# Moving h, queries, keys and y to other SBUF offsets, with two local reorderings and two adds on GpSimd, in a two-layer decoder trunk

## The chip, the cores and the metric

The kernel runs on one core of a Trainium2 chip, in one launch. The metric is the device time of that launch in microseconds (us). Before the change it is 455.19 us, the median of three executions (455.1, 455.19 and 544.2 us). The five engines are called PE (matrix multiply; PEld is its weight load), DVE (VectorE), ACT (ScalarE), POOL (GpSimd) and SP (SyncE, which here issues most DMAs).

## The reference

A trunk of two layers on x of 256 tokens by 1024 channels, all in float32. Each layer takes h = rmsnorm(x) * (1 + scale) + shift, where scale, shift and gate come from c through a matrix (`ada_w`), runs a mixer, and adds gate * y to x. Layer 0 of the reference (here "layer 1") is sparse attention, layer 1 ("layer 2") is an mLSTM:

```python
for i in range(2):
    shift, scale, gate = jnp.split(c @ ada_w[i] + ada_b[i], 3, axis=-1)
    h = rmsnorm(x, norm_g[i]) * (1.0 + scale[:, None, :]) + shift[:, None, :]
    y = nsa_mixer(h, ...) if i == 0 else mlstm_mixer(h, ...)
    x = x + gate[:, None, :] * y
return rmsnorm(x, final_g)
```

`nsa_mixer` projects h to queries (16 heads of 64), six key and value sets (4 groups of 64), gate logits and z. One key set and one value set are compressed: blocks of 32 tokens, each with a position row added (`blocks + pe`), go through a small network. Three attention branches (compressed, selected, sliding; at 256 tokens the last two are causal attention over their own keys and values) are mixed by sigmoid gates, multiplied by silu(z) and projected by `w_out`. `mlstm_mixer` projects h to q, k (with a causal convolution), v, two gates, an output gate and z, runs a gated linear recurrence and projects again.

## The kernel before

**Precision.** A float32 product is made of three matmuls on `float32r` operands. Each factor is split into a high part (rounded by ACT, L165) and a low part (the rest, by DVE, L170); the three are high x high, high x low and low x high. For h these parts are `hh` and `hl`, each 128 partitions x 8 x 256 (8 blocks of 128 channels, 256 tokens). For weights they are `wh` and `wl`, tiles of 1024 columns in rings of six.

**Stream.** SP loads the weights in pieces of up to 512 KB into a ring of ten `raw` tiles (L88) in one fixed order; a piece is issued as soon as the tile that it takes has been read for the last time. `split_next` splits the next piece.

**Layer 1** is written in program order for PE, ACT, DVE and SP (`manual_schedule`); POOL is not in that list. `first_phase` makes the columns of scale and shift from `ada_w`, modulates h block by block (L440, L448) and multiplies each block with the weights of queries and keys: L476, 336 matmuls, the weights stationary, 256 columns of h moving. `evac_cmp` copies the keys and values to be compressed into tiles E and `embed` adds the position rows (L546): two adds for each of E[0] and E[1], all four on DVE. `nsa` finishes the projections: `gemm_tok` (L566 to L568: h stationary, weights moving), `gemm_ws` (L1674 to L1676: weights stationary, 256 columns of h moving), `hidden` (L602: the network of the compressed tokens). Attention runs in eight units n. `S(n)` makes scores (L970 with 256 columns and L974 with 512, queries stationary, keys moving) and DVE turns them into a masked minimum form (L984); `softmax(n)` takes the exponentials on ACT (L996); `factors` and `scaled(n, j)` apply the gates on DVE (L1004 to L1013); `T_pair(n, j)` transposes on PE (L1026) and ACT copies the result out (L1028, tile PT); `PV(n)` multiplies with the values (L1048, L1040). The four `z_steps` are 48 `gemm_ws` matmuls each. `gate_steps` makes half of the residual gate in four steps: rows on PE (L227), a copy on ACT (L938), a matmul on PE (L941), an add on DVE (L944). `cmp_tokens(a)` transposes the compressed scores on PE (L735) into PSUM bank 3, and DVE reads them out (L736); both calls use that bank. y takes the place of the queries, and `out_mm` (L881, 96 matmuls with 512 columns of weights moving, y stationary) makes the output projection.

**The turn and layer 2.** `turn` adds the residual, makes the second h into the same tiles and begins layer 2 (L1279). Layer 2 uses `gemm_tok` with 512 columns, `gemm_ws` for q and k, and in `project` the final product L1165 (y stationary, 512 or 256 columns of weights moving). Its order is set by the framework's scheduler.

**Before the first product** `warm(9)` and `idle` run matmuls whose results nobody reads. `idle` (L255) multiplies a zeroed tile `quiet` with itself 12 times: `float32r`, 512 columns, the stationary part 64, 96, 160, 192, 224 and 384 bytes (mod 512) behind the moving part, twice each.

Of the kernel before, what the change touches and what calls it, by code (L numbers as in the profile page):

```python
# [7 lines left out]
F32 = mybir.dt.float32  # L8
F32R = mybir.dt.float32r
# [3 lines left out]
OP = mybir.AluOpType  # L13
# [10 lines left out]
class Kernel:  # L24
# [225 lines left out]

    def idle(self, w, gaps, i=7):
        z = self.quiet
        b = self.bank(i)
        for c in gaps:
            self.nc.tensor.matmul(b[:, 0:w], z[:, 512 + c : 512 + c + P], z[:, 0:w], start=True, stop=True)  # L255

    def setup(self):
        nc, t, pc = self.nc, self.t, self.pc
        self.x = self.T(pc, [P, 2, D])
        self.hh = self.T(pc, [P, KC, SEQ], F32R)  # L260
        self.hl = self.T(pc, [P, KC, SEQ], F32R)
        xr = t["x"][0].rearrange("(a p) d -> p a d", p=P)
# [10 lines left out]
        nc.vector.memset(still, 0.0)  # L273
        self.quiet = self.T(self.p1, [P, KC * SEQ], F32R, tag="xT")
        nc.vector.memset(self.quiet[:, 0:1024].bitcast(F32), 0.0)
        self.warm(9)
# [72 lines left out]


    def layer1(self):
        nc, t, pc, p1 = self.nc, self.t, self.pc, self.p1
# [49 lines left out]
    def first_phase(self, place):  # L402
# [4 lines left out]
        nc.tensor.transpose(bt[:, 0:32], self.prc, ident[:32, :32])  # L407
        self.idle(512, [n for n in (16, 24, 40, 48, 56, 96) for _ in range(2)])
        pca = self.pca = self.T(pc, [P, 96])
# [6 lines left out]
        xT = self.T(p1, [P, KC, SEQ], tag="xT")  # L416
        ss = self.T(p1, [P, 2], tag="ss2")
        nc.scalar.activation(ss[:, 0:1], self.eps, AF.Sqrt)
        xn = [self.T(p1, [P, D], tag=tag) for tag in ("KH", "KL")]
        for a in range(2):  # L420
            nc.scalar.activation(xn[a], self.x[:, a], AF.Square, accum_out=ss[:, a : a + 1])
# [105 lines left out]
    def evac_cmp(self, accs):  # L527

        nc, p1 = self.nc, self.p1
        self.E, self.F = [], {}  # L530
        for n, acc in enumerate(accs):
            E = self.T(p1, [P, 4, 17, 8], tag="tz", bufs=2)
            self.E.append(E)
            nc.vector.memset(E[:, :, 16], 0.0)
            src = acc.rearrange("p (c x r) -> p c r x", c=2, r=2)
            for half in range(2):
                for par in range(2):
                    dst = E[64 * par : 64 * par + 64, half::2, 0:16].rearrange("p c s u -> p c (s u)")
                    nc.scalar.activation(dst, src[64 * half : 64 * half + 64, :, par], AF.Copy)
            self.embed(n, 0)  # L540

    def embed(self, n, o):

        F = self.F[n, o] = self.T(self.p1, [P, 8, 4, 16], tag="PT", bufs=4)
        pe = self.pca[:, 32 + 16 * n + 8 * o : 40 + 16 * n + 8 * o]
        self.nc.vector.tensor_tensor(F.rearrange("p u g s -> p g s u"), self.E[n][:, :, o : 16 + o], pe.unsqueeze(1).unsqueeze(1).to_broadcast([P, 4, 16, 8]), op=OP.add)  # L546

# [22 lines left out]
    def nsa(self, acc):  # L570
# [70 lines left out]
        hidden(1)  # L641
        for n in range(2):
            self.embed(n, 1)
        vg_block(1)
# [82 lines left out]
        cmp_scores(1)  # L727
        self.scaled(1, 1)
        self.softmax(2, (0,))
        Tc = self.T(p1, [P, 2, 16, 16], tag="tz", bufs=2)  # L730

        def cmp_tokens(a):
            b = self.bank(3)
            for i in range(4):
                nc.tensor.transpose(b[:, i * P : i * P + P], St[i // 2][:, i % 2, a * P : a * P + P], ident)  # L735
            nc.vector.tensor_tensor(Tc[:, a].rearrange("p (i g) s -> p i g s", i=4), b.rearrange("p (i g s) -> p i g s", i=4, g=4)[:, :, :, 0:16],  # L736
                                    self.slc.unsqueeze(2).unsqueeze(3).to_broadcast([P, 4, 4, 16]), op=OP.mult)

        self.PV(0)
        cmp_tokens(0)  # L740
        self.T_pair(1, 0)
        nc.scalar.dma_start(self.gate0, t["ada_b"][0:1, 2048:3072].partition_broadcast(P))
# [59 lines left out]
        g1 = self.gate_steps(1, 3)  # L802
        self.go(g1, 2)

        self.T_pair(3, 0)
        self.go(g1, 2)
        self.split_next()
        self.T_pair(3, 1)
        self.split_next()
        self.factors(4)  # L810
        self.scaled(4, 0)
        self.S(5)
        self.gated(0, 1)
        self.scaled(4, 1)
        self.softmax(5)
        self.PV(3)
        self.gated(1, 0)
        z = self.z_steps(2)
# [385 lines left out]
    def turn(self):  # L1204
        nc, pc, p1, pieces = self.nc, self.pc, self.p1, self.pieces
        halves = [slice(0, 512), slice(512, D)]
        ss = [self.T(pc, [P, 3], tag="ss", bufs=2) for _ in range(2)]
# [182 lines left out]
    def layer2(self):  # L1390
        nc, t, pc, p2, ident = self.nc, self.t, self.pc, self.p2, self.ident
        pcb = self.pcb
        g = nc.gpsimd

        V = self.T(p2, [P, 2, 8, 258], F32R, tag="V")
        VL = [self.T(p2, [P, 2, 258], F32R, tag=f"num{h}") for h in range(8)]
        NUM = {}
        den = self.T(p2, [P, 2, 8])
        g.memset(V.bitcast(F32)[:, :, :, 256:258], 1.0)
# [79 lines left out]
        QK = self.T(p2, [P, 16, SEQ], tag="QK")  # L1479
        ss = self.T(p2, [P, 2, 8])  # L1480

# [236 lines left out]
```

## Time and profile before

| | |
|---|---|
| median of the runs | 455.19 us |
| the profiled execution | 455.72 us |
| its span in the trace | 453.9 us |
| PE, PEld busy | 442.2 us (97%), 373.5 us (82%) |
| DVE, ACT, POOL busy | 328.5 us, 268.0 us, 35.8 us |
| DMA | 95.63 MB, 211 GB/s in the mean |
| granted PE clock | full in all 40 slices |

Times in the trace count from the start of the span. A row of the timeline has the start in us, the time from that start to the end of the last of the merged instructions, engine, line, operation, tiles (out<-in), shape and count; in brackets stand the idle time of the engine before it and what ended it. Matmuls are pipelined: the time of one is its latency, and the pace is the distance from start to start. In the chain of waits a row is start, time and what, and for back-to-back matmuls time over count is the pace.

### The profile page before, as it was taken

Reading aid. Unit: us, or ns where it says so; the run is one execution under the profiler, and the core shown is the slowest. Engines: PE = TensorE matmul, PEld = TensorE weight load, DVE = VectorE, ACT = ScalarE, POOL = GpSimd, SP = SyncE. Lnnn points to the kernel's source line nnn. Section 1 sums busy time; section 2 is a strip of 40 time slices with the busy share of each in tenths; the row PEclk is TensorE's granted clock in tenths of the full one; section 3 lists DMA queues with packets and bytes.
Section 4 is the critical chain, followed back from the end, with each engine's and each line's share of the span. In section 5 each row is a group of like instructions: output and inputs, shape, how many; then the busy total and the mean of one; then the engine's idle time right before and its main releaser. Section 6 shows DMA issues by size and latency. Waiting matters only on the chain.

```text
span 453.9 us, 8341 instructions
## 1 busy us (share of the span) xinstructions
PE 442.2 (97%) x3046; PEld 373.5 (82%) x3046; DVE 328.5 (72%) x761; ACT 268.0 (59%) x527; POOL 35.8 (8%) x100
## 2 busy tenths in 40 slices
PE   8899999999999999999999999999999999999993
PEld 4788998887758877788899889988888888888883
DVE  4555579777869777587998369688986978454635
ACT  4433478675597687356857585555655555454624
POOL 8840022000000000012000000000000000000000
PEclk9999999999999999999999999999999999999999
DMA  8999999982187999897999999887845799740002
GB/s 277 371 330 319 331 357 276 274 315 84 50 269 234 268 240 294 262 202 146 255 142 107 108 303 293 172 153 232 262 141 197 200 225 247 256 139 1 0 1 92
DMA packets 71452, 95.63 MB, mean 211 GB/s; under 512 B 4540, under 2 KB 49908, under 8 KB 71412
## 3 DMA queue, kind: packets, MB, share of 16 engines
q1 hardware_dynamic: 69684, 92.73, 75.7%
q0 software_dynamic: 1392, 1.58, 1.8%
q10 hardware_dynamic: 336, 0.80, 0.5%
q8 instruction: 24, 0.39, 0.4%
q14 instruction: 16, 0.13, 0.1%
HBM read 93.00 MB, written 1.05 MB: 207 GB/s over the span
## 4 chain that ended last, share of the span: by engine, by line
PE 81%; DMA 6%; DVE 4%; ACT 3%; SPq 2%; issue 2%; ACTq 0%
PE bank L568 9%; PE bank L566 8%; PE bank L567 8%; PE bank L1165 8%; PE bank L476 7%; PE bank L1674 5%; PE bank L1675 5%; PE bank L1676 5%; PE bank L881 5%; DMA raw<-in_a_w_in 5%; PE bank L1279 4%; PE bank L227 3%; PE bank L1026 2%; PE bank L1048 2%; SPq L88 2%; PE bank L1512 2%
## 5 line engine op out<-in xcount | busy, mean ns | idle before, releaser
L165 ACT ACTIVATE wh<-raw 128x1024 fp32r<-128x1024 f32 (+5 forms) x126 | 120.8, 977 | 92.4 <-DMA raw<-in_a_w_in 28.5
L170 DVE TENSOR_TENSOR wl<-raw,wh 128x1024 fp32r<-128x1024 f32 (+5 forms) x126 | 139.8, 1123 | 46.9 <-ACT wh L165 46.1
L566 PE MATMUL bank<-wh,one 128*128 128x512 f32 (+2 forms) x208 | 77.0, 371 | 0.0
L567 PE MATMUL bank<-wl,one 128*128 128x512 f32 (+2 forms) x208 | 76.4, 367 | 0.0
L568 PE MATMUL bank<-wh,one 128*128 128x512 f32 (+2 forms) x208 | 76.3, 368 | 0.0
L1674 PE MATMUL bank<-one,wh 128*128 128x256 f32 x208 | 59.6, 286 | 0.0
L1675 PE MATMUL bank<-one,wh 128*128 128x256 f32 x208 | 59.1, 284 | 0.0
L1676 PE MATMUL bank<-one,wl 128*128 128x256 f32 x208 | 59.1, 284 | 0.0
L566 PEld LDWEIGHTS bank<-wh,one 128*128 128x128 f32 x208 | 39.2, 189 | 7.0 <-ACT wh L165 0.4
L568 PEld LDWEIGHTS bank<-wh,one 128*128 128x128 f32 x208 | 39.2, 188 | 6.1
L567 PEld LDWEIGHTS bank<-wl,one 128*128 128x128 f32 x208 | 39.2, 189 | 5.9
L1674 PEld LDWEIGHTS bank<-one,wh 128*128 128x128 f32 x208 | 39.8, 191 | 1.4 <-issue 0.8
L1675 PEld LDWEIGHTS bank<-one,wh 128*128 128x128 f32 x208 | 39.9, 192 | 0.1
L1676 PEld LDWEIGHTS bank<-one,wl 128*128 128x128 f32 x208 | 39.8, 191 | 0.0
L476 PE MATMUL bank<-one,wh 128*128 128x256 f32 x224 | 30.9, 285 | 0.9 <-ACT one L440 0.9
L476 PEld LDWEIGHTS bank<-one,wh 128*128 128x128 f32 x224 | 28.3, 191 | 1.8 <-ACT one L440 1.3
L996 ACT ACTIVATE Pr<-Pr,mn 128x128 f32<-128x128 f32 (+1 forms) x64 | 28.2, 448 | 2.4 <-DVE mn L984 2.4
L1165 PE MATMUL bank<-wl,QK 128*128 128x512 f32 (+1 forms) x80 | 28.2, 353 | 0.0
L1165 PE MATMUL bank<-wh,V 128*128 128x512 f32 (+1 forms) x80 | 28.0, 350 | 0.0
L1165 PE MATMUL bank<-wh,QK 128*128 128x512 f32 (+1 forms) x80 | 28.0, 350 | 0.0
L1493 DVE SCALAR_TENSOR_TENSOR conv<-bank,one,conv 128x255 f32<-128x255 f32 (+2 forms) x48 | 20.3, 475 | 2.1 <-ACT conv L1488 2.1
L984 DVE CUSTOM_DVE_ANT_0 Pr<-bank,one 128x128 f32<-128x128 f32 (+1 forms) x64 | 18.4, 354 | 4.3 <-PE bank L970 4.3
(325 smaller groups left out, 762.4 us busy)
## 6 DMA issues: line engine op xcount, KB each, us to landing
raw<-in_b_w_in SPq DMA_DIRECT2D x62, 512.0 KB, 8.0
raw<-in_ada_w SPq DMA_DIRECT2D x34, 512.0 KB, 6.0
raw<-in_b_w_out SPq DMA_DIRECT2D x16, 512.0 KB, 5.7
raw<-in_a_w_in SPq DMA_DIRECT2D x12, 512.0 KB, 8.1
Q<-in_ada_w SPq DMA_DIRECT2D x8, 512.0 KB, 7.0
raw<-in_a_cmp_w SPq DMA_DIRECT2D x8, 512.0 KB, 8.5
raw<-in_a_w_in SPq DMA_DIRECT2D x16, 256.0 KB, 4.1
raw<-in_a_w_out SPq DMA_DIRECT2D x16, 256.0 KB, 8.6
```

Of the source, the lines that this page charges most:

```text
L165: self.nc.scalar.activation(v(hi), src, AF.Copy)
L170: self.nc.vector.tensor_sub(v(lo), src, v(hi).bitcast(F32))
L476: nc.tensor.matmul(out, w[:, ch * P : ch * P + P], h[:, kk], start=(kk == 0 and m == 0 and ch % 2 == 0), stop=(kk == 7 and m == 2), skip_g ...
L566: nc.tensor.matmul(out, self.hh[:, kk, sl], wh, start=first, stop=False, skip_group_check=True)
L567: nc.tensor.matmul(out, self.hh[:, kk, sl], wl, start=False, stop=False, skip_group_check=True)
L568: nc.tensor.matmul(out, self.hl[:, kk, sl], wh, start=False, stop=last, skip_group_check=True)
L881: nc.tensor.matmul(out, l[:, sl], w[:, c0:c1], start=(k == 0 and m == 0), stop=(k == 7 and m == 2), skip_group_check=True)
L996: self.nc.scalar.activation(v, v, AF.Exp, bias=mn[:, a, br, j : j + 1], scale=-1.0, accum_out=sm[:, a, br, j : j + 1])
L1165: ins = nc.tensor.matmul(out, l[:, sl], w[:, c0:c1], start=(k == 0 and m == 0), stop=(k == N - 1 and m == 2), skip_group_check=True)
L1674: nc.tensor.matmul(out, wh, self.hh[:, kk], start=first, stop=False, skip_group_check=skip)
L1675: nc.tensor.matmul(out, wh, self.hl[:, kk], start=False, stop=False, skip_group_check=skip)
L1676: nc.tensor.matmul(out, wl, self.hh[:, kk], start=False, stop=last, skip_group_check=skip)
```

## The change

Four things are done. Where the lines of code move, the profile's line numbers of the changed kernel differ by a few from those of before.

1. **Offsets.** `hh` and `hl` become two views of one tile `hbuf`, 80 columns longer than the two; layer 1 uses it from column 0, layer 2 from column 80 (`h_views`). Small tiles are padded, or made earlier, so that other tiles shift. The addresses in the two built programs give the distance from the moving to the stationary operand, mod 512 bytes:

| matmuls | columns moving | before | changed |
|---|---|---|---|
| L476 (336), `gemm_ws` of layer 1 (48 for keys, 192 in `z_steps`) | 256 | 256 | 64 |
| `gemm_tok` of layer 1, values (48) | 256 | 256 | 448 |
| `gemm_tok` of layer 1, 304 columns (48) | 304 | 64, 256, 384 | 64, 256, 448 |
| all h products of layer 2, L1279 among them | 256, 512 | 256 | 256 |
| L970 (32), L974 (32): keys against queries | 256, 512 | 0 | 256 |
| L881 (96): y against weights | 512 | 320 (72), 0 (24) | 256 |
| L1165 (144): y against weights | 512 | 448 (96), 0 (48) | 256 |
| L1165 (96) | 256 | 448 (64), 0 (32) | 256 |

2. **Start.** `idle` and the zeroing of its tile on DVE (L275) go; `warm(6)` stands in its place, six bf16 matmuls of 512 columns.

3. **Position rows.** The two second adds of `embed` (o = 1) go from DVE, where they stood in `nsa` behind `hidden(1)`, to POOL, right behind the first two.

4. **Two orders in layer 1.** `scaled(1, 1)` goes behind `cmp_tokens(0)`. In the second gate half, `go(g1, ...)` runs one step before `T_pair(3, 0)`, one behind `T_pair(3, 1)` and two behind `PV(3)`, and `S(5)` goes ahead of `T_pair(3, 1)`.

```diff
     def setup(self):
-        self.hh = self.T(pc, [P, KC, SEQ], F32R)
-        self.hl = self.T(pc, [P, KC, SEQ], F32R)
+        self.hbuf = self.T(pc, [P, 2 * KC * SEQ + 80], F32R)
+        self.h_views(0)
...
-        self.quiet = self.T(self.p1, [P, KC * SEQ], F32R, tag="xT")
-        nc.vector.memset(self.quiet[:, 0:1024].bitcast(F32), 0.0)
+    def h_views(self, c0):
+        n = KC * SEQ
+        self.hh, self.hl = (self.hbuf[:, c0 + n * m : c0 + n * m + n].rearrange("p (k t) -> p k t", k=KC) for m in range(2))
     def first_phase(self, place):
-        self.idle(512, [n for n in (16, 24, 40, 48, 56, 96) for _ in range(2)])
+        self.warm(6)
...
-        ss = self.T(p1, [P, 2], tag="ss2")
+        ss = self.T(p1, [P, 56], tag="ss2")[:, 0:2]
...
+        self.T(p1, [P, 64])
     def evac_cmp(self, accs):
-            self.embed(n, 0)
+            self.embed(n, 0, nc.vector)
+        for n in range(2):
+            self.embed(n, 1, nc.gpsimd)
     def nsa(self, acc):
         hidden(1)
-        for n in range(2):
-            self.embed(n, 1)
...
         cmp_scores(1)
-        self.scaled(1, 1)
         self.softmax(2, (0,))
...
         cmp_tokens(0)
+        self.scaled(1, 1)
         self.T_pair(1, 0)
...
         g1 = self.gate_steps(1, 3)
-        self.go(g1, 2)
+        self.go(g1, 1)
         self.T_pair(3, 0)
-        self.go(g1, 2)
+        self.S(5)
         self.split_next()
         self.T_pair(3, 1)
+        self.go(g1, 1)
         self.split_next()
         self.factors(4)
         self.scaled(4, 0)
-        self.S(5)
...
         self.PV(3)
+        self.go(g1, 2)
     def turn(self):
+        self.h_views(80)
     def layer2(self):
+        den = self.T(p2, [P, 64])[:, 0:16].rearrange("p (a h) -> p a h", a=2)
         V = self.T(p2, [P, 2, 8, 258], F32R, tag="V")
-        den = self.T(p2, [P, 2, 8])
+        ss = self.T(p2, [P, 32])[:, 0:16].rearrange("p (a h) -> p a h", a=2)
...
-        ss = self.T(p2, [P, 2, 8])
```

**PE around the second gate half and S(5).** Rows are line, operation, tiles and size. Before, from the second transpose group of `T_pair(3, 0)` (the first L1026) on:

```order
L1026 MATMUL bank_1844<-one_19_94,Pr_1671 128x128 x3
L941 MATMUL bank_1850<-adaA_1836,one_21_99 128x512
L1026 MATMUL bank_1869<-one_19_94,Pr_1672 128x128 x3
L1026 MATMUL bank_1875<-one_19_94,Pr_1672 128x128 x3
L970 MATMUL bank_1897<-KH_972,Q_1106 128x256
L970 MATMUL bank_1897<-KL_973,Q_1106 128x256
L970 MATMUL bank_1897<-KH_972,Q_1106 128x256
L970 MATMUL bank_1897<-KL_973,Q_1106 128x256
L974 MATMUL bank_1898<-KH_972,Q_1106 128x512
L974 MATMUL bank_1898<-KL_973,Q_1106 128x512
L974 MATMUL bank_1899<-KH_972,Q_1106 128x512
L974 MATMUL bank_1899<-KL_973,Q_1106 128x512
```

Changed, from the same transposes on (L1025, L969, L973 and L1047 are the former L1026, L970, L974 and L1048):

```order
L1025 MATMUL bank_1834<-one_16_91,Pr_1663 128x128 x3
L969 MATMUL bank_1840<-KH_968,Q_1102 128x256
L969 MATMUL bank_1840<-KL_969,Q_1102 128x256
L969 MATMUL bank_1840<-KH_968,Q_1102 128x256
L969 MATMUL bank_1840<-KL_969,Q_1102 128x256
L973 MATMUL bank_1841<-KH_968,Q_1102 128x512
L973 MATMUL bank_1841<-KL_969,Q_1102 128x512
L973 MATMUL bank_1842<-KH_968,Q_1102 128x512
L973 MATMUL bank_1842<-KL_969,Q_1102 128x512
L1025 MATMUL bank_1879<-one_16_91,Pr_1664 128x128 x3
L1025 MATMUL bank_1885<-one_16_91,Pr_1664 128x128 x3
L1047 MATMUL bank_1795<-PT_1832,one_189_970 64x256
```

The eight score matmuls went ahead of the six transposes of `T_pair(3, 1)`; the first matmul of `PV(3)` now follows those transposes at once, and the gate matmul (L941, now L940) stands behind `PV(3)`, just ahead of `z_steps(2)`.

**DVE around the compressed tokens.** Before: the eight scalings of unit 1 (L1013) and the two reads of bank 3 (L736).

```order
L1013 TENSOR_SCALAR Pr_1341<-Pr_1341,f_1503 128x128
L1013 TENSOR_SCALAR Pr_1341<-Pr_1341,f_1503 128x256
L1013 TENSOR_SCALAR Pr_1341<-Pr_1341,f_1503 128x128
L1013 TENSOR_SCALAR Pr_1341<-Pr_1341,f_1503 128x256
L1013 TENSOR_SCALAR Pr_1342<-Pr_1342,f_1503 128x128
L1013 TENSOR_SCALAR Pr_1342<-Pr_1342,f_1503 128x256
L1013 TENSOR_SCALAR Pr_1342<-Pr_1342,f_1503 128x128
L1013 TENSOR_SCALAR Pr_1342<-Pr_1342,f_1503 128x256
L736 TENSOR_TENSOR tz_1529<-bank_1539,one_49_189 128x256
L736 TENSOR_TENSOR tz_1529<-bank_1558,one_49_189 128x256
```

Changed (L1012 and L733 are the same two):

```order
L1012 TENSOR_SCALAR Pr_1333<-Pr_1333,f_1495 128x128
L1012 TENSOR_SCALAR Pr_1333<-Pr_1333,f_1495 128x256
L1012 TENSOR_SCALAR Pr_1333<-Pr_1333,f_1495 128x128
L1012 TENSOR_SCALAR Pr_1333<-Pr_1333,f_1495 128x256
L733 TENSOR_TENSOR tz_1517<-bank_1527,one_46_186 128x256
L1012 TENSOR_SCALAR Pr_1334<-Pr_1334,f_1495 128x128
L1012 TENSOR_SCALAR Pr_1334<-Pr_1334,f_1495 128x256
L1012 TENSOR_SCALAR Pr_1334<-Pr_1334,f_1495 128x128
L1012 TENSOR_SCALAR Pr_1334<-Pr_1334,f_1495 128x256
L733 TENSOR_TENSOR tz_1517<-bank_1550,one_46_186 128x256
```

The read of the first half of the compressed scores went ahead of the last four scalings.

**POOL between the two zero fills and the key copies.** Before (the L560 rows are DMAs, which copy keys to the other half of the partitions):

```order
L764 MEMSET adaA_1628 128x512
L764 MEMSET adaA_1629 128x512
L560 DMA KH_972<-KH_972 64x2x256 x2
L560 DMA KL_973<-KL_973 64x2x256 x2
L560 DMA KH_972<-KH_972 64x2x256 x2
```

Changed:

```order
L762 MEMSET adaA_1620 128x512
L762 MEMSET adaA_1621 128x512
L546 TENSOR_TENSOR PT_940<-tz_924,one_50_202 128x64x8
L546 TENSOR_TENSOR PT_942<-tz_932,one_50_202 128x64x8
L560 DMA KH_968<-KH_968 64x2x256 x2
L560 DMA KL_969<-KL_969 64x2x256 x2
```

The two adds stand on POOL ahead of the four key-copy DMAs of the first key set. What follows from these moves on the other engines: on DVE the 16 instructions that read the scores of S(5) (L984, now L983) go ahead of the four weight splits (L170) that stood in front of them, and the second add of the gate half (L944, now L943) goes behind `scaled(4, 1)`; on ACT the second gate copy (L938, now L937) goes behind the four copies of `T_pair(3, 0)` and `T_pair(3, 1)` (L1028). Layer 2 keeps its order.

More of the change, by code (lines that the diff above doesn't have):

```diff
@@ L249, in warm @@
             self.nc.tensor.matmul(b, self.still[:, 0:P], self.still, start=True, stop=True)
[L251 to L255, printed above, removed]
     def setup(self):
@@ L539, in evac_cmp, with embed @@
                     nc.scalar.activation(dst, src[64 * half : 64 * half + 64, :, par], AF.Copy)
-            self.embed(n, 0)
-    def embed(self, n, o):
+            self.embed(n, 0, nc.vector)
+        for n in range(2):
+            self.embed(n, 1, nc.gpsimd)
+    def embed(self, n, o, eng):
         F = self.F[n, o] = self.T(self.p1, [P, 8, 4, 16], tag="PT", bufs=4)
         pe = self.pca[:, 32 + 16 * n + 8 * o : 40 + 16 * n + 8 * o]
-        self.nc.vector.tensor_tensor(F.rearrange("p u g s -> p g s u"), self.E[n][:, :, o : 16 + o], pe.unsqueeze(1).unsqueeze(1).to_broadcast([P, 4, 16, 8]), op=OP.add)
+        eng.tensor_tensor(F.rearrange("p u g s -> p g s u"), self.E[n][:, :, o : 16 + o], pe.unsqueeze(1).unsqueeze(1).to_broadcast([P, 4, 16, 8]), op=OP.add)
     def dup_split(self, K, br, acc):
```

## The prediction

> **What bounds the kernel now.** I read the profile's page first: span, busy shares and the timeline in 40 slices (one digit for 11.3 us).
>
> ```profile
> span 453.9 us, 8341 instructions
> PE 442.2 (97%) x3046; PEld 373.5 (82%) x3046; DVE 328.5 (72%) x761; ACT 268.0 (59%) x527; POOL 35.8 (8%) x100
> DMA  8999999982187999897999999887845799740002
> ```
>
> PE is busy for 97% of the span. So two things can shorten the kernel: a PE wait that goes, or a smaller distance from one matmul to the next. The digits of DMA add the limit: nines up to about 90 us, then a gap around 110. What feeds PE differs before and after that gap. The chain and the timeline show it at its edge (start, time, what):
>
> ```profile
> 71.37 12.14 DMA raw<-in_a_w_in
> 83.59 1.06 ACT L165 ACTIVATE wh<-raw 128x1024 fp32r<-128x1024 f32 x1 [4.68 <-DMA raw<-in_a_w_in]
> 84.69 1.23 DVE L170 TENSOR_TENSOR wl<-raw,wh 128x1024 fp32r<-128x1024 f32 x1 [1.82 <-ACT wh L165]
> 84.09 0.28 PE L970 MATMUL bank<-KH,Q 128*128 128x256 f32 x1
> 96.47 1.07 PE L1026 MATMUL bank<-one,Pr 128*128 128x128 f32 x6 [0.73 <-DVE Pr L1013]
> ```
>
> A weight piece lands at 83.51. ACT has waited 4.68 us for it, DVE 1.82 us for ACT, and DVE's queue from there on (the splits, the reads of the first scores, the scalings L1013) ends in a PE wait of 0.73 us at 96.47. Up to that point the transfers set the time: a faster PE waits longer there. Behind it the largest PE waits are these two, each a single instruction:
>
> ```profile
> 133.29 1.13 PE L941 MATMUL bank<-adaA,one 128*128 128x512 f32 x2 [0.69 <-ACT adaA L938]
> 111.07 0.66 PE L735 MATMUL bank<-one,y 128*128 128x128 f32 x4 [0.60 <-DVE tz L736]
> ```
>
> Apart from these PE runs back to back to the end, so there a nanosecond per matmul counts.
>
> **Paces.** The distance from start to start depends on the shape and, in these rows, on the offset. First and last start of evenly spaced stretches (for L476, L974 and the bf16 probes, a chain or merged row):
>
> ```profile
> 33.54 8.50 PE bank L476 x71
> 443.97 0.28 PE L1165 MATMUL bank<-wh,QK 128*128 128x256 f32 x1
> 446.68 0.28 PE L1165 MATMUL bank<-wh,V 128*128 128x256 f32 x1
> 224.37 0.39 PE L567 MATMUL bank<-wl,one 128*128 128x512 f32 x1
> 229.35 0.39 PE L568 MATMUL bank<-wh,one 128*128 128x512 f32 x1
> 183.11 0.40 PE L881 MATMUL bank<-wl,Q 128*128 128x512 f32 x1
> 188.24 0.40 PE L881 MATMUL bank<-wh,Q 128*128 128x512 f32 x1
> 439.13 0.40 PE L1165 MATMUL bank<-wh,QK 128*128 128x512 f32 x1
> 118.58 0.92 PE bank L974 x4
> 9.24 1.03 PE L249 MATMUL bank<-y 128*128 128x512 bf16 x4
> ```
>
> - 256 columns at offset 256 (L476): 8.50 / 71 = 119.7 ns. At 448 and 0 (the tail of L1165, 23 distances): 2.71 / 23 = 117.8 ns.
> - 512 columns at 256 (layer 2, 22 distances): 4.98 / 22 = 226.4 ns. At 320 (L881, 22): 5.13 / 22 = 233.2. At 448 and 0 (L1165, 21, from 439.13 to 443.97): 230.5. At 0 (L974): 0.92 / 4 = 230. bf16, which has half the bytes: (1.03 - 0.38) / 3 = 216, with the last one's latency of about 0.38 taken off.
>
> So 256 is the best offset seen for 512 columns, but not for 256 columns. The trace has no 256-column product at 64.
>
> **Offsets, late part.** *Known pairs.* L881: 72 matmuls go from 320 to 256, 72 x 6.8 ns = -0.49 us. L974: 32 x 3.6 = -0.12. L1165: 144 x 4.1 = -0.59 with 512 columns, and 96 x 1.9 = +0.18 with 256 columns (448 and 0 to 256): -0.41. *Unknown: 64 for 256 columns.* Of such products, 192 in `z_steps` lie behind 96.47. Bounds per matmul: a gain of 119.7 - 216 / 2 = 11.7 ns (all that it exceeds half a bf16 product) to a loss of 6.8 ns (the worst difference between two offsets above). I take the nearest row, the 256-column product that isn't at 256: a gain of 1.9 ns, 192 x 1.9 = -0.36. Sum late: -1.38.
>
> **Offsets, early part.** 336 products L476 and 48 for keys, 384 x 1.9 = 0.73 us, all ahead of 96.47. I count nothing: the transfers hide it, and the wait of 0.73 should grow to about 1.4. If that cover were gone, it would be -0.73. The 96 `gemm_tok` products of layer 1 (448 for 256) change by +-4 ns at most, 0.4 us, under the same cover.
>
> **`cmp_tokens`.** The chain is: transposes (L735), DVE's read of bank 3, the second transposes.
>
> ```profile
> 108.75 1.93 DVE L1013 TENSOR_SCALAR Pr<-Pr,f 128x128 f32<-128x128 f32 x8
> 110.59 0.42 DVE L736 TENSOR_TENSOR tz<-bank,one 128x256 f32<-128x256 f32 x1
> ```
>
> The read (0.42) stood behind eight scalings that took 1.93 us; now it stands behind four and starts near 109.8, when the first transposes end. The wait of 0.60 goes: -0.60. Late next are the other four scalings, by the 0.42 of the read, and behind them T_pair(1, 1), which has the second transposes and the `gemm_ws` after them as cover.
>
> **Gate half and S(5).**
>
> ```profile
> 131.72 0.87 PE L1026 MATMUL bank<-one,Pr 128*128 128x128 f32 x6
> 136.41 1.52 PE L1048 MATMUL bank<-PT,one 128*64 128x256 f32 x16
> 137.76 1.03 PE L1040 MATMUL bank<-one,one 128*64 128x256 f32 x8
> 139.07 0.28 PE L1676 MATMUL bank<-one,wl 128*128 128x256 f32 x1
> 135.06 2.56 DVE L170 TENSOR_TENSOR wl<-raw,wh 128x512 fp32r<-128x512 f32 x4
> 167.43 0.87 PE L1026 MATMUL bank<-one,Pr 128*128 128x128 f32 x6
> 168.24 1.84 PE L1048 MATMUL bank<-PT,one 128*64 128x256 f32 x16
> 170.00 0.66 PE L1693 MATMUL bank<-one,adaA 128*128 128x128 f32 x4
> L984 DVE CUSTOM_DVE_ANT_0 Pr<-bank,one 128x128 f32<-128x128 f32 (+1 forms) x64 | 18.4, 354 | 4.3 <-PE bank L970 4.3
> ```
>
> The matmul L941 waited 0.69 us for ACT's copy; now it comes some 4 us later, behind `PV(3)`, and the copy, though behind four PT copies, is long done: -0.69. In its place PV(3) (L1048) follows the transposes at once and must wait for ACT to copy their result. A unit in which this is already so is at 167.43: its PV took 170.00 - 168.24 = 1.76 us, against 137.76 - 136.41 = 1.35 for PV(3) before. So +0.41 (bounds 0, and 1.1 if both copies queue). Behind it PE holds the rest of PV(3), L941 and `z_steps(2)`, and DVE waits for these. Net -0.28.
>
> On DVE the reads of S(5) go ahead of four splits: eight reads of 0.354, 2.8 us, of which the third has to wait until T_pair(3, 1) has read the tile that it writes, near 134.4. So the splits start near 136.2 instead of 135.06, and the first is ready about 136.9. PE reads it (L1676) at 139.07 before, now about 138.4: 1.5 us of cover. If that were gone it would cost the remainder of 1.1 us.
>
> **Position rows.**
>
> ```profile
> 78.37 2.02 DVE L546 TENSOR_TENSOR PT<-tz,one 128x512 f32<-128x512 f32 x2
> 199.97 1.66 POOL L1197 TENSOR_TENSOR one<-one,y 128x512 f32<-128x512 f32 x1 [123.01 <-DVE y L1196]
> 201.12 1.06 DVE L1197 TENSOR_TENSOR one<-one,y 128x512 f32<-128x512 f32 x1
> 202.55 0.68 DVE L1270 TENSOR_TENSOR one<-tz,one 128x512 fp32r<-128x512 f32 x1
> 68.08 2.25 DVE L170 TENSOR_TENSOR wl<-raw,wh 128x1024 fp32r<-128x1024 f32 x2
> 70.60 0.28 PE L1676 MATMUL bank<-one,wl 128*128 128x256 f32 x1
> 66.29 1.31 POOL L560 DMA_DIRECT2D KH<-KH  x2 [7.88 <-ACT KH L555]
> KH<-KH POOLq DMA_DIRECT2D x4, 128.0 KB, 6.8
> ```
>
> DVE is freed of 2.02 us, but then it waits 1.82 us for ACT and the transfer at 84.69, so nothing is gained. On POOL an add of this size took 1.66 us, two 3.3. They stand ahead of the key copies (four DMAs, 2 x 1.31 us of issue from 66.29, 6.8 us each to land): landed by 76 before, by 79 at the worst, read at 84.09. Zero, if DVE isn't held up meanwhile (a rival below).
>
> **Start.** The probes go and six bf16 products stand there. PE waits for DVE at the end of both:
>
> ```profile
> 8.39 0.64 PE L227 MATMUL bank<-raw,one 128*32 128x128 f32 x16 [0.24 <-DVE rq_y L215]
> ```
>
> So zero; DVE's zero fill of 128x1024 comes off its own chain, with at most the 0.4 us that the transfers then take back.
>
> **Sum.** -1.38 - 0.60 - 0.28 = -2.26 us. The profiled execution took 455.72 (span 453.9 and 1.8 around it): 453.46. It lay 0.53 above the median of the three runs, 455.19, so the median should be 452.9. That is 0.5% faster; 2% is 9.1 us, about what a measurement of this kernel can tell from no change.
>
> **Rivals.**
>
> *The offset does nothing.* The paces differ by shape and place in the program (what is loaded next, which banks), not by the offset. For it: even the 119.7 and 117.8 stand in different layers. Against it: L881 is the same loop as a 512-column product of layer 2 and slower by 6.8 ns. Then only the two waits count, -0.88: 455.72 - 0.88 - 0.53 = 454.3.
>
> The Trainium skill ("TensorE: Matmul & The Clock Gate", Part 2, What happens when you issue a matmul) says that PE has two independent SBUF read ports and that loading the next weights takes no read bandwidth from the running product. By that rule this rival is what comes. The trace doesn't agree well: 226.4 against 233.2 at one shape.
>
> *The adds on POOL hold up DVE.* While POOL added (199.97 to 201.63), a DVE add that read two SBUF tiles took 1.06 us, beside 0.68 for the same size just after. If the two new adds each hold back DVE's splits, which stand close there, by their whole 1.66, PE's next weights come 3.3 us late. The first of the two splits from 68.08 is ready near 69.2 and first read at 70.60, a lead of some 1.3; with 0.73 of wait at 96.47 that leaves +1.3 on the forecast, 454.2. The Trainium skill ("SBUF — State Buffer", SBUF: two separate sides) calls the port pair of the two engines an exclusive lock for a whole instruction; those 1.06 us agree.
>
> *64 is a bad place.* If 64 costs 6.8 ns, as 320 does against 256, then the 192 late products lose 1.31 us and the 384 early ones 2.61, of which 0.73 goes into the wait at 96.47. With the other offsets (-1.02) and the waits (-0.88): 1.31 + 1.88 - 1.90 = +1.29, 456.5, slower than before. It decides from 4.6 ns on, where 0.576 x - 0.73 = 1.90. Against it: nothing at 256 columns lies above 119.7.
>
> *64 is much better.* Half of the 11.7, 6 ns: 0.79 us more in the late part, and of the early 2.3 us half gets through, because earlier reads also free `raw` tiles earlier for the stream: 452.9 - 0.8 - 1.15 = 451.0.
>
> **How the numbers follow.** Forecast 0.55, no effect of the offset 0.17, POOL 0.10, 64 bad 0.07, 64 much better 0.11. The range takes in the first three and the last, and the bounds of the wait of PV(3) (-0.4, +0.7): 450.4 to 455.6; it leaves out the bad 64 and the ends of the bounds. No case reaches 2%: within 2% 0.96, and 0.02 on either side for what no row shows.
>
> **What would show it.** Right: the 71 L476 of the chain at about 8.37 us; the 36 L881 of a stretch shorter by 0.16 to 0.25; no wait at the former L735 and L941; a new PE wait of some 0.4 at PV(3) on ACT's PT; the wait near 96 about 1.4 long. Wrong: L476 at 8.50 or more (no effect, or a bad place); a wait near 96 that stays at 0.7 with everything earlier (the early part isn't the transfers'); DVE splits over 1.3 us beside the POOL adds with a PE wait behind them; or PE waits at `z_steps(2)` for its weights.

## The result and the profile after

The changed kernel takes 452.6 us (median of 5 executions), against 455.1 before (5 executions): ratio 0.9946, 95% interval 0.9929 to 0.9963, that is 2.5 us or 0.5% less. One execution of each five (2458.2 and 544.2 us) was disturbed and is left out of the ratio. The profiled execution took 451.9, 0.7 under its median, so its trace flatters the change: 3.8 us lie between the two traces, 2.5 between the medians. Which part of the 3.8 is the change's is the main question of the experiments.

The first lines of the page:

```profile
span 450.1 us, 8331 instructions
PE 438.0 (97%) x3040; PEld 369.6 (82%) x3040; DVE 326.5 (73%) x758; ACT 268.3 (60%) x527; POOL 39.1 (9%) x102
```

PE is 4.2 us less busy, at the same share. The list of PE's waits (us in total, times, longest):

```profile
PE bank L227 <- DMA raw<-in_ada_w: 2.3, 1, 2.3
PE bank L249 <- DVE y L267: 1.2, 1, 1.2
PE bank L227 <- DMA Q<-in_ada_w: 0.6, 1, 0.6
PE bank L474 <- ACT one L438: 0.5, 2, 0.3
PE bank L227 <- DVE xT L927: 0.3, 1, 0.3
```

The three waits that the prediction named (at the former L1026, L735 and L941) are gone. The new 2.3 us stand at the start: with the shorter warm-up PE is idle earlier and waits at the same product L227, which now starts at 8.90 us instead of 8.39. The wait of 0.3 on `xT` (at 120.69) is new as well; it is taken up with the two orders at the end.

The paces, from the chain of waits (start, time, what):

```profile
33.26 8.06 PE bank L474 x71
58.62 5.80 PE bank L474 x49
179.26 8.38 PE bank L880 x36
```

and the last of these before:

```profile
182.84 8.54 PE bank L881 x36
```

L474 (formerly L476), now 64 bytes from its weights: 8.06 / 71 = 113.5 ns, where it was 119.7. But this is a fast stretch: the 49 from 58.62 take 5.80 / 49 = 118.4. Over all distances between neighbours in the trace the mean is 114.8, against 119.6 before; the z steps have 115.6 against 119.6. The 36 L880 (formerly L881) are 0.16 shorter, as 24 products x 6.8 ns. The two orders, first PE around the compressed tokens:

```profile
106.42 1.01 DVE L1012 TENSOR_SCALAR Pr<-Pr,f 128x128 f32<-128x128 f32 x4
107.58 0.42 DVE L733 TENSOR_TENSOR tz<-bank,one 128x256 f32<-128x256 f32 x1 [0.15 <-PE bank L732]
107.92 1.00 DVE L1012 TENSOR_SCALAR Pr<-Pr,f 128x128 f32<-128x128 f32 x4
108.06 0.66 PE L732 MATMUL bank<-one,y 128*128 128x128 f32 x4
```

DVE's read now waits for PE (0.15) instead of PE for it, and the second transposes come without a wait. Then the gate half and S(5), PE, ACT and DVE:

```profile
128.92 0.87 PE L1025 MATMUL bank<-one,Pr 128*128 128x128 f32 x6
131.04 0.82 PE L1025 MATMUL bank<-one,Pr 128*128 128x128 f32 x6
131.78 1.68 PE L1047 MATMUL bank<-PT,one 128*64 128x256 f32 x14
133.13 0.38 PE L1039 MATMUL bank<-one,one 128*64 128x256 f32 x1
134.48 1.12 PE L940 MATMUL bank<-adaA,one 128*128 128x512 f32 x2
135.68 0.28 PE L1676 MATMUL bank<-one,wl 128*128 128x256 f32 x1
132.38 0.59 ACT L937 ACTIVATE adaA<-bank 128x512 f32<-128x512 f32 x1
131.89 0.29 DVE L983 CUSTOM_DVE_ANT_0 Pr<-bank,one 128x128 f32<-128x128 f32 x1 [1.07 <-PE bank L1025]
133.69 2.49 DVE L170 TENSOR_TENSOR wl<-raw,wh 128x512 fp32r<-128x512 f32 x4
```

From the transposes of T_pair(3, 0) to the third product of `z_steps(2)` PE does the same work in another order: 139.07 - 131.72 = 7.35 us before, 135.68 - 128.92 = 6.76 now. The copy L937 ends at 132.97 and the matmul L940 comes at 134.48: no wait. DVE's third read of S(5) waits 1.07 us for the transposes, as worked out, and the first split is ready near 134.3, 1.4 us before PE reads it at 135.68. The position rows, on POOL and DVE:

```profile
62.79 4.07 POOL L546 TENSOR_TENSOR PT<-tz,one 128x512 f32<-128x512 f32 x2 [5.41 <-ACT tz L537]
64.32 1.51 DVE L546 TENSOR_TENSOR PT<-tz,one 128x512 f32<-128x512 f32 x1 [0.46 <-ACT tz L537]
67.10 2.25 DVE L170 TENSOR_TENSOR wl<-raw,wh 128x1024 fp32r<-128x1024 f32 x2
66.81 1.33 POOL L560 DMA_DIRECT2D KH<-KH  x2
```

Before, the same DVE add was:

```profile
65.41 1.09 DVE L546 TENSOR_TENSOR PT<-tz,one 128x512 f32<-128x512 f32 x1 [0.47 <-ACT tz L539]
```

The two adds took 4.07 us on POOL, more than the 3.3 estimated. DVE's own add beside them took 1.51 us instead of 1.09, but the splits at 67.10 start behind POOL's end and take their usual 2.25. The key copies are issued 0.5 us later than before.

**A ruler for the traces.** Between the second transposes of unit 0 (the former L1026, at 96.47 before) and the end PE waits for no transfer, so this *late part* should scatter little; what lies ahead of it follows the transfers. I measure the late part from that point to the start of the last product: 446.68 - 96.47 = 350.2 us before (both rows stand in the prediction) and, by these two rows, 442.82 - 94.37 = 348.45 after, so -1.75.

```profile
94.37 1.07 PE bank L1025 x6
```

```profile
442.82 0.28 PE L1164 MATMUL bank<-wh,V 128*128 128x256 f32 x1
```

Kernels below with the same late part check how sharp the ruler is.

### The profile page after: what moved, and what is told of

It is laid out like the page before. It is cut to its first block, busy times and chain, and to the rows that moved or that the text cites. A ratio compares the mean times of both kernels' runs of the same rounds, so it can differ in the third digit from the quotient of the medians.

```text
span 450.1 us, 8331 instructions
## 1 busy us (share of the span) xinstructions
PE 438.0 (97%) x3040; PEld 369.6 (82%) x3040; DVE 326.5 (73%) x758; ACT 268.3 (60%) x527; POOL 39.1 (9%) x102
## 4 chain that ended last, share of the span: by engine, by line
PE 89%; DVE 4%; DMA 2%; SPq 2%; ACT 1%; issue 0%; ACTq 0%
PE bank L566 10%; PE bank L568 9%; PE bank L567 9%; PE bank L1164 8%; PE bank L474 8%; PE bank L1674 5%; PE bank L1675 5%; PE bank L1676 5%; PE bank L880 5%; PE bank L227 4%; PE bank L1279 4%; PE bank L1047 2%; PE bank L1025 2%; DMA Q<-in_ada_w 2%; PE bank L1512 2%; PE bank L602 2%
## 5 line engine op out<-in xcount | busy, mean ns | idle before, releaser
L170 DVE TENSOR_TENSOR wl<-raw,wh 128x1024 fp32r<-128x1024 f32 (+5 forms) x126 | 140.0, 1124 | 46.0 <-ACT wh L165 45.2
L1674 PE MATMUL bank<-one,wh 128*128 128x256 f32 x208 | 59.5, 286 | 0.0
L1675 PE MATMUL bank<-one,wh 128*128 128x256 f32 x208 | 58.8, 282 | 0.0
L1674 PEld LDWEIGHTS bank<-one,wh 128*128 128x128 f32 x208 | 39.6, 190 | 1.3 <-issue 0.6
L1675 PEld LDWEIGHTS bank<-one,wh 128*128 128x128 f32 x208 | 39.6, 190 | 0.3 <-issue 0.2
L474 PE MATMUL bank<-one,wh 128*128 128x256 f32 x224 | 29.8, 280 | 0.5 <-ACT one L438 0.5
L474 PEld LDWEIGHTS bank<-one,wh 128*128 128x128 f32 x224 | 27.3, 188 | 1.3 <-ACT one L438 0.9
L983 DVE CUSTOM_DVE_ANT_0 Pr<-bank,one 128x128 f32<-128x128 f32 (+1 forms) x64 | 18.5, 353 | 6.9 <-PE bank L969 5.8
```

The source lines that it names most:

```text
L170: self.nc.vector.tensor_sub(v(lo), src, v(hi).bitcast(F32))
L474: nc.tensor.matmul(out, w[:, ch * P : ch * P + P], h[:, kk], start=(kk == 0 and m == 0 and ch % 2 == 0), stop=(kk == 7 and m == 2), skip_g ...
L1674: nc.tensor.matmul(out, wh, self.hh[:, kk], start=first, stop=False, skip_group_check=skip)
L1675: nc.tensor.matmul(out, wh, self.hl[:, kk], start=False, stop=False, skip_group_check=skip)
```

## The experiments

Theory A (formed on the two traces): the 64-byte offset gains about 4.8 ns for each of 576 products, and the gain of the early 384 passes on too, because PE's own progress frees the tiles that the stream waits for. Theory B (the prediction): the transfers hide the early part. Theory C: the offset does nothing.

**Layer 1's h alone.** The kernel before, with

```
-        self.hh = self.T(pc, [P, KC, SEQ], F32R)
-        self.hl = self.T(pc, [P, KC, SEQ], F32R)
+        self.hbuf = self.T(pc, [P, 2 * KC * SEQ + 128], F32R)
+        self.h_views(48)
...
     def turn(self):
+        self.h_views(0)
```

> The kernel before with one edit: layer 1's h lies 48 columns further on, so that its 256-column products have their weights 64 instead of 256 bytes on (mod 512); every other offset, order and queue stays. Theory A (the changed kernel's trace shows 115 ns for these products instead of 120): the gain of about 4.8 ns counts for all 576 products, the early 384 too, because PE's own progress frees the tiles that the stream waits for: 455.1 - 2.6 = 452.5. Theory B (as predicted: the transfers hide the early part): only the 192 late ones count, 455.1 - 0.9 = 454.2. Theory C (the offset does nothing, the profiles differ by scatter and the orders): 455.1.

Measured: 453.21, ratio 0.996 (0.9946 to 0.9974), so -1.8 us; late part 349.40, -0.80. C falls, and the interval of -1.2 to -2.5 us just leaves out B's -0.9 and A's -2.6. The late part bears out the pace (192 x 5.0 ns = 0.96). The other 1.0 lies in the early part, between B's 0 and A's 384 x 4.8 ns = 1.84.

**Everything but layer 1's h.** The changed kernel with h back at 256:

```
     def setup(self):
-        self.h_views(0)
+        self.h_views(80)
```

> The changed kernel with layer 1's h back at 256 bytes from its weights, all else as changed. Theory A: it gives back what the offset brought in both parts, 452.6 + 2.6 = 455.2 if nothing else gained, and 454.2 if the two waits bring their 0.9 on their own. Theory B: 452.6 + 0.9 = 453.5. Theory C: 452.6.

Measured: 453.82, ratio 0.9976 (0.9967 to 0.9984), -1.1 us; late part 348.74, -1.46. The time lies between B's 453.5 and A's 454.2. The two halves of the change, 1.8 and 1.1, add up to the whole of 2.5 within the intervals.

**The orders.** The changed kernel with

```
+        self.scaled(1, 1)
         self.softmax(2, (0,))
...
         cmp_tokens(0)
-        self.scaled(1, 1)
...
-        self.go(g1, 1)
+        self.go(g1, 2)
         self.T_pair(3, 0)
-        self.S(5)
+        self.go(g1, 2)
...
-        self.go(g1, 1)
...
         self.scaled(4, 0)
+        self.S(5)
...
         self.PV(3)
-        self.go(g1, 2)
```

> The changed kernel with the two orders of layer 1 as before (the scalings of unit 1 ahead of the compressed tokens, the second gate half ahead of its transposes, S(5) behind). If the waits removed are worth what the profile of before showed, 0.6 and 0.3 us: 453.5. If they only moved (each came back as another wait): 452.6.

Measured: 453.4, ratio 0.9963 (0.995 to 0.9977); late part 349.10, 0.65 longer than with the orders changed. The ratio's interval overlaps that of the changed kernel, so it is the ruler and the waits that show the orders' worth. PE's waits in layer 1's attention:

```profile
PE bank L1024 <- DVE Pr L1011: 0.8, 1, 0.8
PE bank L939 <- ACT adaA L936: 0.7, 1, 0.7
PE bank L733 <- DVE tz L734: 0.6, 1, 0.6
```

The last two are the waits that the orders had taken away, as long as before. The first stands at the transposes near 96 us, which the orders don't touch (see "The kernel before once more").

**The pace of every offset.** The kernel before with other probes at the start:

```
-        self.idle(512, [n for n in (16, 24, 40, 48, 56, 96) for _ in range(2)])
+        for w in (256, 512):
+            self.idle(w, [8 * n for n in range(16) for _ in range(12)])
```

> The kernel before with the 12 probes at the start replaced by 12 for each of the 16 offsets 0, 32, ... 480 bytes, once with 256 and once with 512 columns moving (zeros). If the offset alone sets the pace: about 115 ns at 64 and 120 at 256 for 256 columns; 226 at 256, 233 at 320 and 230 at 0 and 448 for 512 columns. If place, tiles or data set it: one pace for all 16 offsets. The time is some 60 us longer than before either way.

Mean distance in ns of the last ten of each twelve, from the trace's starts (zeros moving; the offsets from 256 to 480 repeat those from 0 to 224 within 0.8 at 256 columns and, but for 0 itself, exactly at 512):

| offset mod 256 | 0 | 32 | 64 | 96 | 128 | 160 | 192 | 224 |
|---|---|---|---|---|---|---|---|---|
| 256 columns | 118.9 to 119.7 | 118.6 | 117.7 | 117.3 | 119.7 | 119.3 | 117.8 | 117.9 |
| 512 columns | 226.7 to 229.2 | 233.1 | 233.3 | 234.0 | 231.6 | 233.7 | 229.2 | 233.2 |

So the offset alone does set a pace, with a period of 256 bytes: for 256 columns 96 and 64 are the fastest, 0, 128 and 160 the slowest, for 512 columns 0 is fast and nearly all else slow. But for 256 columns the difference is 2 ns here, not 5.

**Queries, keys and y alone.** The changed kernel with h at 256 and orders, adds and start as before; what remains against before are the tiles' places:

```
+        ss = self.T(p1, [P, 56], tag="ss2")[:, 0:2]
+        self.T(p1, [P, 64])
...
+        den = self.T(p2, [P, 64])[:, 0:16].rearrange("p (a h) -> p a h", a=2)
+        ss = self.T(p2, [P, 32])[:, 0:16].rearrange("p (a h) -> p a h", a=2)
```

> The changed kernel with layer 1's h at 256 again, both orders, the adds and the start as before: against before only queries, keys and y lie elsewhere (output products of both layers and scores at 256). By the prediction's terms (0.49 + 0.12 + 0.41): 1.0 below before. By the probes of all offsets, where the pace repeats every 256 bytes, 0 counts as 256: then only the 72 products at 320 and the 96 at 448 gain, 72 x 6.8 + 96 x 2.5 ns = 0.7 below, less the 64 products of 256 columns that were at 448 (+0.1): 0.6 below. If the offsets of these products do nothing: equal to before.

Measured: 454.6, ratio 0.9997 (0.9989 to 1.0006); late part 349.86, -0.34. The -1.0 of the prediction is excluded by the ratio as by the ruler, and the -0.6 that the probes gave lies just outside the ratio's interval (-0.5 at most).

**The adds.** The changed kernel with

```
-        for n in range(2):
-            self.embed(n, 1, nc.gpsimd)
...
         hidden(1)
+        for n in range(2):
+            self.embed(n, 1, nc.vector)
```

> The changed kernel with the two second position adds back on DVE, behind the second hidden layer, all else as changed. As predicted (the adds cost and bring nothing): as fast as the changed kernel, 2.5 below before. Rival: freeing DVE of 2.0 us is what took the wait near 96 us away, so it comes back here: 0.7 slower than the changed kernel, 1.8 below before. Rival on the other side: on GpSimd they delay the key copies and with them the weight stream: 3.0 or more below before.

Measured: 452.36, ratio 0.9952 (0.994 to 0.9964); late part 348.53. The same as the changed kernel. The wait near 96 us is back in this trace, as the first rival expected:

```profile
PE bank L1025 <- DVE Pr L1012: 1.1, 1, 1.1
```

This execution (453.57) was the slowest of the five, but the median isn't longer for the adds.

**The start.** The changed kernel with the probes and their zero fill back:

```
...
-        self.warm(6)
+        self.idle(512, [n for n in (16, 24, 40, 48, 56, 96) for _ in range(2)])
```

> The changed kernel with the 12 float32r probes and the zero fill of their tile back in place of the six bf16 products. As predicted (PE waits at 8.4 us anyway, nothing hangs on it): as the changed kernel, 2.5 below before. Rival: the changed kernel begins its first real product 0.5 us later than before (8.90 against 8.39), and that is the start's doing: then this one is up to 0.5 us faster, 3.0 below before.

Measured: 452.12, ratio 0.9947 (0.9934 to 0.9961); late part 348.42. The same again. These three kernels (this one, the one with the adds undone, the changed one) have late parts of 348.42, 348.53 and 348.45: by these three the ruler is good to about 0.1 us. Their points near 96 lie at 96.15, 95.74 and 94.37, though their medians hardly differ: the early part of one execution says little.

**The kernel before once more.**

> The kernel before, profiled once more. If the wait of 0.73 us near 96 us belongs to the kernel: it is there again, and that point lies near 96.5. If it is scatter of the transfers: another wait there or none, that point moved by 0.5 us or more, and the stretch behind it as long as before (350.20 us to the start of the last product) within 0.1.

Measured: 454.65. The row of the second transposes, and PE's longest waits:

```profile
95.43 1.05 PE L1026 MATMUL bank<-one,Pr 128*128 128x128 f32 x6
```

```profile
PE bank L249 <- DVE y L273: 1.2, 1, 1.2
PE bank L941 <- ACT adaA L938: 0.7, 1, 0.7
PE bank L735 <- DVE tz L736: 0.6, 1, 0.6
PE bank L476 <- ACT one L440: 0.6, 2, 0.4
```

The wait of 0.73 on DVE is not there, the point lies 1.04 earlier, and the late part is 350.18, as before. So that wait comes and goes between executions of one kernel, while those at L941 and L735 belong to it. Of the twelve traces of this study without new probes, four have the wait: 0.73 before, 0.22 with queries, keys and y alone, 0.84 with the orders undone, 1.11 with the adds on DVE; in the other eight it is under 0.1. Whether the adds on POOL make it rarer (one of seven traces with them, three of five without) is not shown.

**Layer 2's products at 64 as well.** The changed kernel, with

```
...
+        s = 16 * (m in self.ws)
-        return [self.pw.tile([P, 1024], F32R, name=self.nm(tag), tag=tag, bufs=self.WBUF) for tag in ("wh", "wl")]
+        return [self.pw.tile([P, 1088], F32R, name=self.nm(tag), tag=tag, bufs=self.WBUF)[:, s : s + 1024] for tag in ("wh", "wl")]
...
             unit(1024 + 256 * h)
+            self.ws |= set(range(len(self.queue) - 4, len(self.queue)))
```

and two pairs of small tiles of layer 1 sharing a place, to make the room.

> The changed kernel with layer 2's stationary weights 64 bytes further on inside their tiles (the tiles 256 bytes longer), so that its 384 products of 256 columns have 64 instead of 256 (mod 256), while the weights that move stay at 0 (mod 256). The tiles of all rings shift by multiples of 256 bytes. If the offset mod 256 alone sets the pace: 384 x 4.4 ns = 1.7 us faster than the changed kernel, 4.2 below before. If mod 512 matters (half of the products lie at 320 or 0): 0.8 faster at most, or slower. If layer 2's products gain only what the zero-filled probes showed (119.0 to 117.7): 0.5 faster.

> The kernel of ws2_shifted once more, as the neighbour of late_only_64: ratio to before 0.993 as before, and the stretch behind the transposes near 96 us as long as in ws2_shifted (347.75 us) within 0.1, whatever the start does.

Measured: 451.97, ratio 0.9929 (0.9916 to 0.9942), and 451.67, ratio 0.9934 (0.9918 to 0.9949), the two fastest medians of the study; its intervals still touch the changed kernel's. Late part 347.75 and 347.46, that is 0.7 and 1.0 less. Layer 2's 256-column products went from 119.8 to 117.8 ns, 384 x 2.0 = 0.77: the gain of the zero probes, not the 4.4 of layer 1. The two runs of one program lie 0.29 apart on the ruler, more than the 0.1 expected, so 0.3 is the safer figure for it. That mod 256 is what counts is borne out: half of these products lie at 320, and yet all 369 distances in either trace are 117 to 119 ns.

The same two traces show something else. Here are the third and the 36th of the first z products, in the first run and then in the second:

```profile
96.50 0.28 PE L1679 MATMUL bank<-one,wl 128*128 128x256 f32 x1
100.39 0.28 PE L1679 MATMUL bank<-one,wl 128*128 128x256 f32 x1
96.28 0.28 PE L1679 MATMUL bank<-one,wl 128*128 128x256 f32 x1
100.02 0.28 PE L1679 MATMUL bank<-one,wl 128*128 128x256 f32 x1
```

That is 3.89 / 33 = 117.9 ns in one and 3.74 / 33 = 113.3 in the other, for the same products at the same addresses. Layer 1's products at 64 have these two paces in all eight traces that have such products, each held through a stretch of some ten to 70 products: in the changed kernel 332 distances are 113 or 114 ns and 185 are 117 to 119.

**The early products back at 256.** As the kernel just above, with

```
-        self.h_views(0)
+        self.h_views(80)
...
-        s = 16 * (m in self.ws)
+        s = 16 * (m in self.ws or self.queue[m][0] == "z")
```

> As ws2_shifted (all 256-column products 64 bytes from their weights, mod 256), but with layer 1's h at 256 for the 384 products that lie ahead of the transposes near 96 us, and the 192 of the z steps kept at 64 by the same shift of their weights. Behind 96 us nothing changes. Theory A (measured so far: kernels with h at 64 are on average 0.9 us of a possible 1.84 earlier at that point): 0.9 us slower than ws2_again, the kernel ws2_shifted run once more beside it. Theory B (as predicted, the transfers hide the early part): equal to ws2_again. Theory C (PE sets the early part fully): 1.84 us slower.

Measured: 452.86, ratio 0.9953 (0.9938 to 0.9968), against 0.9934 for its neighbour: 0.9 us slower, as A expected, but with an uncertainty of 1.0, so that alone doesn't exclude B. The late part is 347.56, like its neighbour's.

**All kernels together.** The early gain is the ratio's gain less the ruler's (us against before; the ratio times some 454.8):

| kernel | early products at | whole | late | early |
|---|---|---|---|---|
| h alone at 64 | 64 | -1.8 | -0.80 | -1.0 |
| changed | 64 | -2.5 | -1.75 | -0.7 |
| orders undone | 64 | -1.7 | -1.10 | -0.6 |
| adds on DVE | 64 | -2.2 | -1.67 | -0.5 |
| start undone | 64 | -2.4 | -1.78 | -0.6 |
| layer 2 shifted, twice | 64 | -3.2, -3.0 | -2.45, -2.74 | -0.8, -0.3 |
| h at 256 | 256 | -1.1 | -1.46 | +0.4 |
| queries, keys, y alone | 256 | -0.1 | -0.34 | +0.2 |
| early back at 256 | 256 | -2.1 | -2.64 | +0.5 |

Each early figure is uncertain by some 0.5, but all seven with the early products at 64 are negative (mean -0.6) and all three at 256 positive (mean +0.4, where 0 was due; why isn't known). So, by the difference of the two, about 1.0 of the possible 384 x 4.8 = 1.84 gets through. A's reason would be that SP waits for tiles to come free. Before the change it waited, over the whole span, for DVE's splits, which read them (us in total, times, longest):

```profile
SPq L88 <- DVE wl L170: 148.3, 57, 11.9
```

That a faster PE shortens these waits is argued and not shown.

**Probes that step**, to see whether the address pattern makes the layer 1 pace of 115 ns:

```
...
+        for c in range(0, 128, 8):
+            for n in range(24):
+                k = n % 3
+                self.nc.tensor.matmul(self.bank(7)[:, 0:256], ..., self.quiet[:, 256 * k : 256 * k + 256], start=True, stop=True)
```

> The kernel before with probes of 256 columns at the start, 24 for each of the 16 offsets 0, 32, ... 480, that step as the real products do: three moving blocks in turn, another weight block every three products (zeros). If the address pattern makes the 115 ns of the real products at 64: 115 here at 64 and 320, 120 at 0 and 256. If it is the data or something else: 117.7 as with the probes that repeat one address.

This failed as an experiment: it asks for the bank anew for each product, which puts a wait between any two. The row of one weight load shows it:

```profile
99.88 0.29 PEld L411 LDWEIGHTS bank<-xT 128*128 128x128 f32 x1 [0.35 <-PE bank L411]
```

The products stand 440 ns apart at first and then, with the granted clock at five tenths, 640, whatever the offset. That tells nothing on the pattern.

## Why the prediction was right, point by point

The time was right (452.9 forecast, 452.6 measured), but that it came so close is in part luck: the known pairs were forecast too large, the offset of layer 1 and its early part too small, and the errors nearly cancel.

- **"Offsets, early part ... I count nothing: the transfers hide it": wrong.** About -1.0 us passes. The argument rested on the wait of 0.73 us at 96.47 in one trace, and the second trace of the same kernel doesn't have it. That the wait "should grow to about 1.4" failed too: the changed kernel has none there. Something is taken, since 1.0 of 1.84 arrives; which of the early waits takes the rest stays open. The rival "64 is much better" came nearest in mechanism: it had half of the early gain pass, because earlier reads free `raw` tiles earlier.
- **The 64-byte offset, 1.9 ns: mis-sized.** It is 4 to 5 ns in layer 1 (119.6 to 114.8 and 115.6), between the bounds (a loss of 6.8, a gain of 11.7). For the 192 late products the ruler gives -0.80, not -0.36. The value taken, from products at 448, is what the zero probes and layer 2 give at 64 (2 ns). Layer 1 gains more than twice that because more than half of its products run at the second pace of 113.3, which neither the zero probes nor layer 2 show. What sets the pace of a stretch is open: the addresses alone don't, as the two traces of one program show, and the probe that should have told more was lost.
- **Known pairs, -1.02: mis-sized**, -0.34 by the ruler. The base of 226.4 ns was a stretch of 22 even distances; all 512-column products of `gemm_tok` at 256 average 228, and L1165 after the change, at 256, still 229.3 (230.3 and 231.9 before, 230.9 in the mean). The 32 L974 went from 0 to 256, which is the same place mod 256: 232.1 before, 232.6 after. By the traces L881 gains 72 x 4.2 = 0.30 (234.3 to 230.1), and L1165 gains 144 x 1.6 = 0.23 with 512 columns and loses 96 x 1.3 = 0.12 with 256 (117.7 to 119.0).
- **The two orders, -0.88: right.** The ruler gives -0.65 (undone from the changed kernel) and -1.12 (349.86 less 348.74, orders with adds and start). The new wait at PV(3), +0.41, came smaller: L1047 to L1039 are 133.13 - 131.78 = 1.35, as before, and the whole stretch became 0.59 shorter (7.35 to 6.76) where a wait of 0.69 went, so some 0.1 came in its place. What the prediction didn't have is the wait of PE at L227 on DVE's `xT`, 0.34 at 120.69: the traces with both orders changed have 0.17 to 0.47 there, the others 0.14 at most.
- **Position rows and start, 0: right**, each shown by its own kernel. The rival in which POOL's adds hold up DVE was right in its mechanism (DVE's add 1.51 instead of 1.09) and wrong in its price, because the splits come behind them. The Trainium skill ("SBUF — State Buffer", SBUF: two separate sides) has an exclusive lock here, which holds up whichever of the two starts second. The trace agrees: the add that was held up by 0.42 us began while a POOL add ran, and at no cost to PE.
- **The rival "the offset does nothing": excluded** (ratio 0.996, upper bound 0.9974, with only the offset changed). In these runs the distance between what moves and what is loaded changes the pace by 2 to 5 ns of 120 and by 7 of 227. The rule of the Trainium skill named beside this rival ("TensorE: Matmul & The Clock Gate", Part 2, What happens when you issue a matmul) has PE's two read ports independent of each other; the measurement differs, and what the cause is was not tested.

The late terms were -1.38 - 0.88 = -2.26 forecast and -1.75 measured; the early term 0 and about -0.7 in the changed kernel's own row. The two errors nearly cancel.

## What to carry to other kernels

A pace must be compared over all instructions of a kind, not over the most even stretch: here one kind had two paces at one offset. Before a tile is moved a probe of all offsets costs one run; with zeros and one repeated address it gave the slower of the two. A wait on a transfer chain that one trace shows may be scatter: a second trace of the same kernel settles that, and a stretch behind the transfers serves as a ruler that is sharper than the total time. A small gain in an early stretch that looks bound by transfers can still pass in part.

## What the runs showed of the hardware

- The pace of float32r products depends on the distance in SBUF between the moving operand and the weights being loaded, with a period of 256 bytes: 117.3 to 119.7 ns at 256 columns and 226.7 to 234.0 at 512, with zeros in both.
- At 64 bytes (mod 256) and 256 columns, layer 1's products run at 113.3 or at 117.8 ns, and two executions of one program differ in which (117.9 and 113.3 for the same 33 distances). Layer 2's and the probes' run at the slower one alone.
- The best offsets for 256 columns (64 and 96) are bad ones for 512 (233.3 and 234.0), so one h can't serve both kinds at their best, unless the weights of one kind are shifted.
- Two adds of 128x512 that took 1.01 us each on DVE took 4.07 together on POOL, and a DVE add beside them 1.51 instead of 1.09.
- In the failed probe, where each product waited for the one before, the granted clock fell to five tenths until those products were done, and their distance went from 440 to 640 ns:

```profile
PEclk7555555555555569999999999999999999999999
```
